# Short convolutions computed at the projection's PSUM tiles, with neighbours' terms accumulated in DRAM, and the last column groups regrouped

## The chip, the cores and the metric

The kernel runs on one core of one Trainium2 chip. The metric is the device time of one execution in microseconds (us); of a kernel the median over its runs is given. All arithmetic is float32; the large matrix products split their operands in two parts (a rounded high part and the rest) and add three products.

## The reference

A two-layer backbone over 2048 tokens of width 1024. Layer 0 is a pooling mixer beside attention; layer 1, which the change concerns, is a Hyena mixer (long convolutions) beside a 2-D Fourier mixing. Cut to what matters:

```python
def short_conv3(u, w, b):
    up = jnp.pad(u, ((0, 0), (1, 1), (0, 0)))
    return up[:, :-2] * w[0] + up[:, 1:-1] * w[1] + up[:, 2:] * w[2] + b

def hyena_mixer(u, conv_w, conv_b, w1, b1, w2, b2, w3, freq, skip):
    uc = short_conv3(u, conv_w, conv_b)                 # 2304 channels
    v, x1, x2 = jnp.split(uc, HY_ORDER + 1, axis=-1)    # 768 channels each
    k = hyena_filters(L, w1, b1, w2, b2, w3, freq)
    z = v.astype(jnp.float32)
    for o, gate_o in enumerate((x1, x2)):
        z = gate_o * (fft_long_conv(z, k[:, o]) + skip[o] * z)
    return z

def odd_mix(h, w_in, w_out, ...):                       # layer 1
    hy_in, hy_gate, fn_in, fn_gate = jnp.split(h @ w_in, ODD_SPLITS, axis=-1)
    yc = hyena_mixer(hy_in, ...)
    yd = fourier_mixer(fn_in, fn_w)
    y = jnp.concatenate([yc * silu(hy_gate), yd * silu(fn_gate)], axis=-1)
    return y @ w_out
```

## The kernel before

**Layout.** Channels lie on the 128 partitions. The 3584 columns of layer 1's input projection are 28 groups `mt` of 128: 0 to 5 are `v`, 6 to 11 `x1`, 12 to 17 `x2`, 18 to 23 the Hyena gate, 24 and 25 the Fourier input, 26 and 27 its gate. Tokens are stored in the order n2 * 128 + n1 for token 16 * n1 + n2, as 16 slots of 128. So a token's neighbours lie in the same column of the slot before and the slot after; only slot 0 and slot 15 have neighbours one column further, in each other. A token block `tb` is four slots, 512 tokens.

**Who orders the work.** The order of the instructions on each engine is written out by a small planner (`Jobs`). `jobs.pe(us)` says how long the matrix products just given will take and lets planned time pass; lanes (`Lane`) hold generators whose `yield us, gap` or `yield event` say how long a piece takes and when the next may come; `jobs.at` gives a function a planned time; `jobs.store` puts a store into SP's queue at the next `jobs.pe`. Planned times only decide the order. On the chip each engine and each DMA queue goes through its own list in order and waits for what an instruction needs. SP's queue carries nearly all loads and stores, POOL's queue those that accumulate (`accum_op=ALU.add`) and some loads.

**Layer 0's end (about 1740 to 2075 us).** `out_half` computes layer 0's output projection; `turn_one` transposes, scales and splits the normalized tokens (`hf`, `ch`); `project0` computes the columns of the four groups FIRST (0, 1, 6, 7) from them, one PSUM bank each, and `keep_cols` copies each bank on ACT into `dev` and stores it to `ud[mt]` in DRAM. Group 0 is treated apart (`first_unit`): its short convolution and the first step of its transform are done at once.

**The projection stage (about 2075 to 2812 us).** 192 steps: six groups of four `mt` (`MGROUPS`), four token blocks, eight blocks of 128 input channels; twelve matrix products a step (L306 to L308), with `dw` (weights) and `dh` (the layer's input) loaded by SP, `dh` three steps ahead (`HL`). After each eighth step `keep_cols` takes the four banks: ACT copies (L1522) or SiLU (L1525) into `dev`, then a store. Between these steps go the long convolutions: twelve units (j, o), each a transform by TensorE matrices and a 16-point transform on DVE (`s1`, `conv_units`, `fft16`), a product with the filter's spectrum (`gK`), and back (`s4`, with the gating of `co`, L1913 and L1917). DVE's part of a unit comes in the order of the units.

**The short convolutions** are done by `conv(n)`, one group after another, on the lane `ctl`: POOL's queue loads the whole group, 1 MB, into `cu` (L1824); ACT computes the middle term with the bias into `co` (L1829) and the first tap into `tap`, half a group at a time in one buffer (L1834); POOL's queue adds `tap` to `co`, SBUF to SBUF (L1837, L1840, L1841); ACT scales `cu` by the last tap in place (L1842) and POOL's queue adds that too (L1844, L1845). `cdone[mt]` releases the gating or the transform that reads `co`. The planned gaps CV0 to CV3 are 14, 12, 8 and 15 us.

**After the projections.** `udone` of the last four groups is set; the Fourier mixing (`hEO`, tables `tab`), the first pass of the output projection for the channels EARLY (added to `x1d` in DRAM from `ox`, L2196), the last units of the long convolutions, and the last pass with the final norm from about 3056 us.

Of the kernel before, what the change touches and what calls it, by code (L numbers as in the profile page):

```python
# [20 lines left out]
P = 128  # L21
D = 1024
# [17 lines left out]
EARLY, LATE = (0, 1, 2, 6, 7), (3, 4, 5)  # L40

# [16 lines left out]
def constants():  # L58
    """Tables that depend on the shapes alone."""
# [58 lines left out]
def sbc(ap, n):  # L118
    """[p, f] -> [p, n, f], the same f for each n."""
    return ap.unsqueeze(1).to_broadcast([ap.shape[0], n, ap.shape[1]])  # L120


def lbc(ap, n):
    """[p, f] -> [p, f, n], each element n times."""
    return ap.unsqueeze(2).to_broadcast([ap.shape[0], ap.shape[1], n])


def fft16(v, X, T, inv, s=None):
    """16-point transforms over the slots of X[p, re/im, 16, C]; T is of the same shape.
# [26 lines left out]
    def stt(out, in0, scalar, op, in1):  # L156
        """in0 already has its factor where s does the products, but for the sign"""
# [28 lines left out]
    def tan(n, *dims):  # L186
        """the slots from n on, times the tangent"""
# [16 lines left out]
    # the second four: slots k * e + b * o for b; 11 and 14 have the other sign  # L204
# [35 lines left out]
def tile_net(ctx, tc, i, k, out, keep=None):  # L240
# [9 lines left out]
    def mv(dst, src, eng=None):  # L250
        """a DMA of float32 words, of either type"""
# [22 lines left out]
    def y1_part(kk):  # L274
        """the place of gated channels of layer 1"""
# [5 lines left out]
    wevd, wod = ([dram(f"w{x}{kk}", (P, 2, D)) for kk in range(KD)] for x in "eo")  # L281
    hdd = dram("hdd", (8, 64, 4, P))
# [30 lines left out]
    class Lane:  # L313
        """pieces for one engine, each of so many us, the next one at least so many later, or after an event"""
# [30 lines left out]
    class Jobs:  # L345
        """the order in which work is given to the engines: matrix products in front, the rest when they are that far"""
# [37 lines left out]
        def until(self, done):  # L384
            """let time pass until done()"""
# [15 lines left out]
    def load_wout(sp, wp, w, kks, dst, gb, wait=4.0, eng=sy, ve=v):  # L401
        """output projection times the gate, in two parts, one tile of rows at a time"""
# [21 lines left out]
    def load_gate(wp, n):  # L424
        """the gate of layer n, the same in every partition"""
# [4 lines left out]
    def rstd_steps(sp, ss, n, tag, scale):  # L430
        """ss [p, n] sums of squares -> 1 / sqrt(ss * scale + eps), with a Newton step after the square root"""
# [13 lines left out]
    def normed_steps(sp, xs):  # L445
        """each slab [p, D] of xs -> each row over its root mean square, in place"""
# [13 lines left out]
    def modulated_steps(sp, pp, xs, gs, sh, emit, lo_eng):  # L460
        """transposed, scaled and shifted, in two parts: emit(m) gives their places"""
# [12 lines left out]
    LASTE, LASTR, GATE2, FOLD1, HALF, SUM0, SUM1, ADDF, FEW, LASTW, IN_C, FFT_N, FFT_LATE, HL, DR, DE, EW0, EW1, SPLIT, SUMMED, QSEL, CV0, CV1, CV2, CV3, COL, NW0, NW1, FIRST_Z, MORE, X0_SQ, X0_STEP, TRAIL, C_EARLY, A_TURN, A_SLOW, A_AHEAD, A_W, A_PACE, LAG0, FOLD, WAIT, AHEAD, LAG, APART, LOW, W_LOAD, W_HIGH, W_LOW, ADDED, SLOW = 0, 0.5, 5, 6, 1.5, 0.2, 1.5, 3, 9, 3.5, 25, 6, 4, 3, 4, 4, 8.0, 2.5, 15, 0.5, 1, 14, 12, 8, 15, 5, 24, 0, 20.0, 8, [7, 7, 11, 11], (0, 0, 0, 0, 2, 2, 2, 2), 11, 1, 2.5, 0.25, 3.5, 4, 1.05, 7, 2, 6.0, 2.5, 5, 5, 2, 6, 6, 4, 8, 1.02  # L474
    # tokens in the order n2 * 128 + n1 for token 16 * n1 + n2
# [5 lines left out]
    FIRST = (0, 1, 6, 7)  # L481
    MGROUPS = [(2, 8, 12, 18), (3, 9, 13, 19), (4, 10, 14, 20), (5, 11, 15, 21), (24, 25, 26, 27), (16, 22, 17, 23)]

    def load_columns(raw, gi, kk, half, eng=sy):
        """128 rows of half of the columns of a group"""
# [5 lines left out]
    with ExitStack() as st, tc.manual_schedule(engines=EVERY):  # L491
# [10 lines left out]
        def load_tb(tb):  # L502
            """a block of tokens, a list of slabs"""
# [14 lines left out]
        def weights(c0, dst):  # L518
            """256 columns of the input projection, in two parts, one tile per 128 rows"""
# [13 lines left out]
        def norm_parts(xs):  # L533
            """the same as normed_steps, in smaller steps"""
# [12 lines left out]
        with ExitStack() as s2:  # L547
# [21 lines left out]
            # the filters' network, on two halves of its input at a time  # L569
# [26 lines left out]
            def load_first(n):  # L596
                """256 columns for the keys, as many for the values"""
# [125 lines left out]
        class Aside:  # L723
            """work that goes between the matrix products, in pieces of so many us of an engine, the next one so many later"""
# [31 lines left out]
        def turn(xs, gs, sh, tiles, lo_eng=(v, v)):  # L756
            """normalized tokens, modulated and turned, in two parts"""
# [12 lines left out]
        def rope_tables(tb):  # L770
            """cos and sin times the norm's gains, for queries and keys"""
# [15 lines left out]
        def heads(raw, ss, nt, tb, nm, dst, col0):  # L787
            """raw [p, nt, 2, HD] in place: ss its sums of squares; normalized over HD, rotated; transposed to dst[head]"""
# [41 lines left out]
        def modulation():  # L830
            """what is left of the modulation: the gate of layer 0, all of layer 1"""
# [51 lines left out]
        def mixer():  # L883
            """the pooling mixer, over halves of n1"""
# [893 lines left out]
    with ExitStack() as st, tc.manual_schedule(engines=EVERY):  # L1778
# [212 lines left out]
        with ExitStack() as ps:  # L1991
# [29 lines left out]
            for mt in MGROUPS[-1]:  # L2021
                udone[mt].t = jobs.now
# [349 lines left out]
```

## Time and profile before

| | |
|---|---|
| median of 3 runs | 3173.34 us (3167.35 to 3176.21) |
| span of the profiled execution | 3162.6 us |
| its own time | not given beside the span; the median lies 10.7 us above the span |
| busy: PE, DVE, ACT, POOL | 2996.1, 2183.2, 1329.8, 1215.5 us |
| DMA | 614.72 MB, mean 194 GB/s |

The span goes from the first to the last instruction of one execution. "Busy" is the time in which an engine ran instructions (matmul ends are modelled); the share of a stage is read from windows of the trace, and who waits for what from the semaphores. `A <- B` in a row of waits means that A's engine stood until B was done. A row of DMA issues gives the tile written and the one read, the queue, the count, the size of one and the median time from issue to landing. q0 is the queue of the DMAs that POOL issues, q1 that of the others.

### The profile page before, as it was taken

How to read it: one execution, taken by the hardware profiler on the slowest of the kernel's cores; microseconds unless marked ns; L12 is line 12 of the kernel's file. 1: busy time of each engine (PE TensorE's matmuls, PEld its weight loads, DVE VectorE, ACT ScalarE, POOL GpSimd, SP SyncE). 2: the span in 40 equal slices, each digit the busy share in tenths (PEclk: the TensorE clock that was granted, in tenths of full speed). 3: DMA queues.
4: the chain of work that ended last, by engine and by line, in shares of the span. 5: the costliest groups of instructions: out<-in, count | busy, mean ns of one | idle time of the engine just before them, and what ended most of it. 6: DMA issues, size and time to landing. Idle time of an engine off the chain costs nothing. (4 is left out here: it accounts for less than half of the span.)

```text
span 3162.6 us, 49927 instructions
## 1 busy us (share of the span) xinstructions
PE 2996.1 (95%) x18121; PEld 2589.2 (82%) x18121; DVE 2183.2 (69%) x4124; ACT 1329.8 (42%) x3130; POOL 1215.5 (38%) x1595
## 2 busy tenths in 40 slices
PE   8999999799999999999999999999989999988799
PEld 4888888699999998999898778777878787874587
DVE  4775437477777777777776443377789797978556
ACT  4444545355555555555556332322323232232123
POOL 3122223027888887878886344001010100101110
PEclk9999999899999999999999999999999999999899
DMA  6466345534444445444443777678899989976875
GB/s 223 157 202 202 125 132 162 182 107 127 121 140 132 128 127 169 121 125 133 117 115 117 250 261 256 242 258 283 275 290 288 293 282 314 275 260 167 233 210 176
DMA packets 425393, 614.72 MB, mean 194 GB/s; under 512 B 140278, under 2 KB 278200, under 8 KB 416698
## 3 DMA queue, kind: packets, MB, share of 16 engines
q1 hardware_dynamic: 399994, 528.43, 51.0%
q0 software_dynamic: 25152, 83.10, 11.2%
q8 instruction: 143, 2.34, 0.3%
q14 instruction: 104, 0.85, 0.1%
HBM read 388.60 MB, written 187.18 MB: 182 GB/s over the span
## 5 line engine op out<-in xcount | busy, mean ns | idle before, releaser
L303 DVE TENSOR_TENSOR pl<-pt,ph 128x512 fp32r<-128x512 f32 (+1 forms) x480 | 299.8, 633 | 137.1 <-ACT ph L300 136.1
L151 DVE TENSOR_TENSOR gB<-gB 128x256 f32<-128x256 f32 (+3 forms) x442 | 351.6, 845 | 51.2 <-ACT gB L1879 47.3
L300 ACT CAST ph<-pt 128x512 fp32r<-128x512 f32 (+1 forms) x480 | 253.5, 556 | 244.7 <-PE pt L1317 242.3
L306 PE MATMUL dacc<-dh,dw 128*128 128x512 f32 x768 | 312.2, 407 | 40.2 <-DMA dh<-h1T 39.5
L1306 ACT ACTIVATE pb<-S,mx 128x512 f32<-128x512 f32 (+1 forms) x480 | 309.7, 656 | 82.7 <-DVE mx L1298 59.4
L307 PE MATMUL dacc<-dh,dw 128*128 128x512 f32 x768 | 304.7, 397 | 0.0
L308 PE MATMUL dacc<-dh,dw 128*128 128x512 f32 x768 | 304.6, 397 | 0.0
L1295 DVE TENSOR_REDUCE mx<-S 128x1 f32<-128x512 f32 (+1 forms) x480 | 279.9, 629 | 18.6 <-DMA kh<-kT0h 14.0
L303 POOL TENSOR_TENSOR wl<-raw,wh 128x256 fp32r<-128x256 f32 x160 | 135.6, 880 | 368.6 <-ACT wh L300 356.7
L1317 PE MATMUL pt<-ident,pb 128*128 128x128 f32 x1728 | 248.0, 275 | 11.2 <-ACT pb L1306 10.9
L151 POOL TENSOR_TENSOR fX<-fT 128x128 f32<-128x128 f32 (+2 forms) x336 | 246.7, 757 | 4.9
L1329 PE MATMUL o<-ph,vh 128*128 128x256 f32 x864 | 233.0, 301 | 1.4 <-ACT ph L300 1.2
L151 POOL TENSOR_TENSOR fT<-fX 128x1024 f32<-128x1024 f32 (+1 forms) x192 | 202.6, 1081 | 49.0 <-ACT fX L1203 44.6
L1317 PEld LDWEIGHTS pt<-ident,pb 128*128 128x128 f32 x1728 | 197.2, 141 | 28.2 <-ACT pb L1306 14.8
L1330 PE MATMUL o<-ph,vl 128*128 128x256 f32 x864 | 216.5, 282 | 1.5 <-DMA vl<-vl 1.5
L306 PEld LDWEIGHTS dacc<-dh,dw 128*128 128x128 f32 x768 | 147.9, 193 | 78.2 <-DMA dh<-h1T 46.7
L306 PE MATMUL S<-kh,qh 128*128 128x512 f32 (+1 forms) x480 | 196.9, 410 | 9.9 <-DMA kl<-kT0l 8.2
L306 PE MATMUL acc<-wh,hh 128*128 128x256 f32 x672 | 197.2, 293 | 3.5 <-ACT qraw L969 2.4
L308 PE MATMUL acc<-wh,hl 128*128 128x256 f32 x672 | 193.1, 287 | 1.2 <-DVE hl L303 0.9
L307 PE MATMUL acc<-wl,hh 128*128 128x256 f32 x672 | 192.8, 287 | 0.9 <-POOL wl L303 0.8
L307 PE MATMUL S<-kl,qh 128*128 128x512 f32 (+1 forms) x480 | 180.4, 376 | 1.1 <-DMA kl<-kT0l 1.0
L308 PE MATMUL S<-kh,ql 128*128 128x512 f32 (+1 forms) x480 | 180.4, 376 | 0.0
(473 smaller groups left out, 7776.5 us busy)
## 6 DMA issues: line engine op xcount, KB each, us to landing
dh<-h1T SPq DMA_DIRECT2D x172, 512.0 KB
dec<-cst_decay_dram SPq DMA_DIRECT2D x96, 256.0 KB
spec<-fX SPq DMA_DIRECT2D x24, 1024.0 KB
dw<-wi SPq DMA_DIRECT2D x48, 512.0 KB
gK<-spec SPq DMA_DIRECT2D x48, 512.0 KB
raw<-in_ev_w_in_dram SPq DMA_DIRECT2D x160, 128.0 KB
u<-dev SPq DMA_DIRECT2D x70, 256.0 KB
cu<-u POOLq DMA_DIRECT2D x17, 1024.0 KB, 8.3
```

Of the source, the lines that this page charges most:

```text
L151: put(out, lambda: v.tensor_tensor(out=out, in0=in0, in1=in1, op=op))
L300: s.copy(hi, src)
L303: lo_eng.tensor_sub(lo, src, hi.bitcast(F32))
L306: pe.matmul(acc, ah, bh, start=first, stop=False)
L307: pe.matmul(acc, ah, bl, start=False, stop=False)
L308: pe.matmul(acc, al, bh, start=False, stop=last)
L1295: v.tensor_reduce(out=B["mx"][:, c : c + 1], in_=S[:, :n], axis=AX.X, op=ALU.max)
L1306: s.activation(B["pb"][:, c * 512 : c * 512 + n], B["S"][c][:, :n], AF.Exp, bias=B["mx"][:, 5:6], accum_out=B["sm"][:, c : c + 1])
L1317: pe.transpose(pt[:, t, :], B["pb"][:, (4 * c + t) * P : (4 * c + t + 1) * P], ident)
L1329: pe.matmul(gr["o"], vh[:, a, :], ph[:, t, :], start=a == 0, stop=False)
L1330: pe.matmul(gr["o"], vl[:, a, :], ph[:, t, :], start=False, stop=False)
```

## The change

The neighbours' terms and the bias are applied to each block of 128 channels by 512 tokens as it leaves PSUM, instead of to a whole group later. Within the block, two slots next to each other are served on DVE; one neighbour at the block's edge is kept in SBUF for the next block (`edges`, `before`), and terms that belong to slots already stored are scaled on ACT (`far`, `low`) and accumulated into `ud[mt]` in DRAM by POOL's queue. The blocks of a group of columns run upwards or downwards in turn (`up`). `conv(n)` is only a load of the finished group. In detail, for groups 2 to 5 and 8 to 17 (comments and docstrings, which the change also removes, and moved blank lines are left out):

```diff
-    MGROUPS = [..., (24, 25, 26, 27), (16, 22, 17, 23)]
+    MGROUPS = [..., (16, 22, 24, 25), (17, 23, 26, 27)]
+    firstd = [dram(f"first{mt}", (P, P)) for mt in range(18)]
-    ... CV0, CV1, CV2, CV3, ... = ... 14, 12, 8, 15, ...
+    ... CV0, CV1, CV2, CV3, CV_N, CV_S, DE_, ... = ... 0.3, 2.5, 6, 10, 5, 1.7, 5, ...

+    def taps(mt):
+        return *(col2[:, 18 * x + mt : 18 * x + mt + 1] for x in range(3)), ud[mt].rearrange("p (a b) -> p a b", a=N2)
+    def add_to(dst, src):
+        g.dma_start(dst, src, accum_op=ALU.add)
     def keep_cols(jobs, ep, mt, acc, tb, up=True):
...
-        if mt < 18 or mt in (24, 25):
+        if 0 < mt < 18:
+            s.copy(ev, acc)
+            convlane[0].add(short_conv(jobs, ep, mt, ev.rearrange("p (a b) -> p a b", a=4), tb, up))
+        elif mt < 18 or mt in (24, 25):
             s.copy(ev, acc)
             jobs.store((ud[mt] if mt < 18 else fid[mt - 24])[:, bl], ev)

+    def short_conv(jobs, ep, mt, u, tb, up):
+        w0, w1, w2, o = taps(mt)
+        n0 = 4 * tb
+        first, final_ = (0, NB - 1) if up else (NB - 1, 0)
+        wn, wf = (w0, w2) if up else (w2, w0)
+        next_, other = (3, 0) if up else (0, 3)
+        own, of = (slice(1, 4), slice(0, 3)) if up else (slice(0, 3), slice(1, 4))
+        yield 0.0, CV0
+        mid = ep.tile([P, 4, P], F32, tag="ev", name="dm")
+        s.activation(mid, u, AF.Identity, bias=..., scale=w1)
+        far = nextfar()
+        s.mul(far, u, wf)
+        yield 0.0, CV_S
+        v.scalar_tensor_tensor(out=mid[:, own], in0=u[:, of], scalar=wn, in1=mid[:, own], op0=ALU.mult, op1=ALU.add)
+        if tb == first:
+            edges[mt] = ep.tile([P, P], F32, tag="eb", name="deb", bufs=4)
+        else:
+            v.tensor_add(mid[:, other], mid[:, other], edges[mt])
+        s.mul(edges[mt], u[:, next_], wn)
+        jobs.lanes[0].took(jobs.now, 0.8)
+        def put():
+            sy.dma_start(o[:, n0 : n0 + 4], mid)
+            if tb == first:
+                sy.dma_start(firstd[mt], far[:, other])
+        def more():
+            x = int(tb == first)
+            if up:
+                add_to(o[:, n0 - 1 + x : n0 + 3], far[:, x:])
+            else:
+                add_to(o[:, n0 + 1 : n0 + 5 - x], far[:, : 4 - x])
+            if tb == final_:
+                to0, to15 = (edges[mt], firstd[mt]) if up else (firstd[mt], edges[mt])
+                add_to(o[:, 0, 1:], to0[:, : P - 1])
+                add_to(o[:, 15, : P - 1], to15[:, 1:])
+                del edges[mt]
+        jobs.at(jobs.now + CV1, 0.0, put)
+        jobs.at(jobs.now + CV2, 0.0, more)
```

`fars` are four such blocks in the room of the former `cu`, used in turn. `ep` has five buffers (`DE_`) instead of four in the projection stage. For the groups 1, 6 and 7 of FIRST, straight from PSUM:

```diff
+        def first_conv(n, mt, u, tb):
+            w0, w1, w2, o = taps(mt)
+            n0 = 4 * tb
+            mid = ep.tile([P, 4, P], F32, tag="ev", name="cm")
+            s.activation(mid, u, AF.Identity, bias=..., scale=w1)
+            low = ep.tile([P, P], F32, tag="cl", name="cl", bufs=3)
+            s.mul(low, u[:, 0], w2)
+            def rest():
+                for to, of, w in ((slice(1, 4), slice(0, 3), w0), (slice(0, 3), slice(1, 4), w2)):
+                    v.scalar_tensor_tensor(out=mid[:, to], in0=u[:, of], scalar=w, in1=mid[:, to], op0=ALU.mult, op1=ALU.add)
+                if tb:
+                    v.tensor_add(mid[:, 0], mid[:, 0], before[n])
+                else:
+                    before[n] = ep.tile([P, P], F32, tag=f"cb{n}", name="cb", bufs=1)
+                s.mul(before[n], u[:, 3], w0)
+                dve.took(jobs.now, 1.4)
+                jobs.store(o[:, n0 : n0 + 4], mid)
+                if tb == 0:
+                    jobs.store(firstd[mt], low)
+                jobs.at(jobs.now + 4.0, 0.0, edge)
+            def edge():
+                if tb:
+                    add_to(o[:, n0 - 1], low)
+                if tb == NB - 1:
+                    add_to(o[:, 0, 1:], before[n][:, : P - 1])
+                    add_to(o[:, 15, : P - 1], firstd[mt][:, 1:])
+            jobs.at(jobs.now + 1.3, 0.0, rest)
-            hf = sp.tile([P, 512], F32, tag="hf", name="hf", bufs=1)
+            hf = sp.tile([P, 4, P], F32, tag="zT", name="hf").rearrange("p a b -> p (a b)")
```

And what reads the result:

```diff
         def conv(n):
             mt = convs[n]
             yield udone[mt]
             yield cdone[convs[n - 1]]
-            u = per.tile([P, N2, P], F32, tag="u", name="cu")
-            QU.dma_start(u, ud[mt].rearrange("p (a b) -> p a b", a=N2))
-            yield 0.0, CV0
             if mt in room:
                 yield room[mt]
             o = cout[mt] = (per if mt < 6 else ct).tile([P, N2, P], F32, tag="ct", name="co")
-            s.activation(o, u, AF.Identity, bias=..., scale=...)
-            ...
-            g.dma_start(o[:, 15, : P - 1], u[:, 0, 1:], accum_op=ALU.add)
+            QU.dma_start(o, ud[mt].rearrange("p (a b) -> p a b", a=N2))
             yield 0.0, CV3
             cdone[mt].t = jobs.now
...
-                if x % GS == 0 and x:
+                if x % GS == CV_N and x > GS:
                     for mt in MGROUPS[gi - 1]:
                         udone[mt].t = jobs.now
...
+            jobs.until(lambda: not edges)
             for mt in MGROUPS[-1]:
                 udone[mt].t = jobs.now
```

More of the change, by code (lines that the diff above doesn't have):

```diff
@@ L40 @@
 EARLY, LATE = (0, 1, 2, 6, 7), (3, 4, 5)
+FIRST = (0, 1, 6, 7)
 BLOCK = [
@@ L479, in tile_net @@
     EVERY = {ET.PE, ET.DVE, ET.Activation, ET.Pool, ET.SP}
-    FIRST = (0, 1, 6, 7)
-    MGROUPS = [(2, 8, 12, 18), (3, 9, 13, 19), (4, 10, 14, 20), (5, 11, 15, 21), (24, 25, 26, 27), (16, 22, 17, 23)]
+    MGROUPS = [(2, 8, 12, 18), (3, 9, 13, 19), (4, 10, 14, 20), (5, 11, 15, 21), (16, 22, 24, 25), (17, 23, 26, 27)]
     def load_columns(raw, gi, kk, half, eng=sy):
@@ L1647, in project0 @@
                         s.copy(u0[0][:, 4 * tb : 4 * tb + 4, :], accs[n].rearrange("p (a b) -> p a b", a=4))
+                    elif n == 0:
+                        keep_cols(jobs, ep, 0, accs[n], tb)
                     else:
-                        keep_cols(jobs, ep, FIRST[n], accs[n], tb)
+                        first_conv(n, FIRST[n], accs[n].rearrange("p (a b) -> p a b", a=4), tb)
                 if 0 in ns:
@@ L1654, in project0 @@
                 jobs.pe(0.65 * len(ns))
+        before = {}
+        def first_conv(n, mt, u, tb):
+            w0, w1, w2, o = taps(mt)
+            n0 = 4 * tb
+            mid = ep.tile([P, 4, P], F32, tag="ev", name="cm")
+            s.activation(mid, u, AF.Identity, bias=col2[:, PK2["cb"] + mt : PK2["cb"] + mt + 1], scale=w1)
+            low = ep.tile([P, P], F32, tag="cl", name="cl", bufs=3)
[20 more added lines that the diff above has]
+            jobs.at(jobs.now + 1.3, 0.0, rest)
         columns = [Event() for _ in range(NB)]
@@ L1828, in conv @@
             o = cout[mt] = (per if mt < 6 else ct).tile([P, N2, P], F32, tag="ct", name="co")
-            s.activation(o, u, AF.Identity, bias=col2[:, PK2["cb"] + mt : PK2["cb"] + mt + 1],
-                         scale=col2[:, 18 + mt : 19 + mt])
-            yield 0.0, 2.2
-            for a in (0, 8):
-                t = sp.tile([P, 8, P], F32, tag="tap", name="tap", bufs=1)
-                s.mul(t, u[:, a : a + 8], col2[:, mt : mt + 1])
-                yield 0.0, 1.2
-                if a == 0:
-                    g.dma_start(o[:, 1:9], t, accum_op=ALU.add)
-                    yield 0.0, CV1
-                else:
-                    g.dma_start(o[:, 9:], t[:, :7], accum_op=ALU.add)
-                    g.dma_start(o[:, 0, 1:], t[:, 7, : P - 1], accum_op=ALU.add)
-            s.mul(u, u, col2[:, 36 + mt : 37 + mt])
-            yield 0.0, CV2
-            g.dma_start(o[:, :15], u[:, 1:], accum_op=ALU.add)
-            g.dma_start(o[:, 15, : P - 1], u[:, 0, 1:], accum_op=ALU.add)
+            QU.dma_start(o, ud[mt].rearrange("p (a b) -> p a b", a=N2))
             yield 0.0, CV3
@@ L1991, in tile_net @@
         with ExitStack() as ps:
-            ep = pool(ps, "d_e", DE)
+            ep = pool(ps, "d_e", DE_)
+            u8 = per.tile([P, N2, P], F32, tag="u", name="far")
+            convlane.append(jobs.lane())
+            fars.extend(u8[:, 4 * x : 4 * x + 4] for x in range(4))
             pm = pool(ps, "d_ps", 1, PSUM)
@@ L2264, in tile_net @@
             jobs.flush()
-            fg = sp.tile([P, D], F32, tag="tap", name="fg", bufs=1)
+            jf = per.tile([P, 2, D], F32, tag="u", name="jk")
+            junk, fg = jf[:, 0], jf[:, 1]
             sy.dma_start(fg, i["final_g"].rearrange("(o d) -> o d", o=1).to_broadcast([P, D]))
-            junk = per.tile([P, D], F32, tag="u", name="jk")
             eps = modc[:, 12:13]
```

12 lines of the change are left out of this document (9 added, 3 removed).

## The prediction

> **What bounds the kernel now.** I read the page's first lines, then one table of stages, then who waits for whom in the stage that the change rewrites, then single rows around the longest stop there.
>
> ```profile
> span 3162.6 us, 49927 instructions
> ...
> PE 2996.1 (95%) x18121; PEld 2589.2 (82%) x18121; DVE 2183.2 (69%) x4124; ACT 1329.8 (42%) x3130; POOL 1215.5 (38%) x1595
> ```
>
> PE is the bound over the whole span: 166.5 us are all that it idles (its matmul ends are modelled, so this is a floor). The change removes no matrix product, so it can only win back idle time and the slow clock that follows it. By stages, in the columns PE, weight loads, DVE, ACT, POOL, granted clock, DMA share, GB/s:
>
> ```profile
> 1740.00:2060.00 320.00, 306.59 (x1483) 252.99 (x1482) 127.44 (x212) 97.44 (x194) 100.77 (x125) 0.98 0.70 251
> 2190.00:2812.00 622.00, 585.14 (x3133) 499.93 (x3131) 514.12 (x852) 182.34 (x231) 60.35 (x75) 0.98 0.91 287
> 2812.00:2945.00 133.00, 118.80 (x506) 78.93 (x507) 108.88 (x190) 35.36 (x58) 11.31 (x14) 0.92 0.71 210
> 2945.00:3056.00 111.00, 94.22 (x422) 75.95 (x420) 64.58 (x108) 25.47 (x46) 25.54 (x31) 0.92 0.90 225
> ...
> 2060.00:2812.00 752.00, 704.00 (x3674) 597.89 (x3672) 619.41 (x1015) 215.75 (x274) 71.16 (x89) 0.97 0.90 284
> ```
>
> The first row is layer 0's output projection with the columns FIRST, the last row the projection stage with most of the long convolutions. It has 48 us of PE idle and a clock of 0.97, which is 0.03 x 752 = 22.6 us more, some of it inside the idle time. From 2812 to 3056 (Fourier mixing, first output pass) PE idles 14.2 + 16.8 = 31.0 us. The waits of the projection stage (us in total, times, longest):
>
> ```profile
> POOL co L1837 <- ACT tap L1834: 215.1, 14, 23.9
> ...
> ACT tap L1834 <- DMA co<-tap: 64.2, 8, 10.9
> DVE co L1913 <- PE go L1904: 51.6, 13, 6.9
> ...
> DVE gB L151 <- ACT gB L1879: 47.3, 5, 19.1
> ...
> PE dacc L306 <- DMA dh<-h1T: 39.5, 18, 8.3
> ```
>
> 39.5 of the 48 us are PE waiting for its moving operand `dh`. Why it is late shows around the longest of these stops (ACT, then SP's queue, then PE):
>
> ```profile
> 2304.45 1.16 ACT L1834 ACTIVATE tap<-cu,col 128x1024 f32<-128x1024 f32 x1 [8.51 <-DMA co<-tap]
> ...
> 2307.55 1.54 ACT L1522 COPY dev<-dacc 128x512 f32<-128x512 f32 x3
> ```
> ```profile
> 2308.14 1.66 SPq L252 DMA_DIRECT2D u<-dev  x3
> ```
> ```profile
> 2168.66 0.79 PE L306 MATMUL dacc<-dh,dw 128*128 128x512 f32 x1 [4.06 <-DMA dh<-h1T]
> ...
> 2327.79 0.79 PE L306 MATMUL dacc<-dh,dw 128*128 128x512 f32 x1 [8.29 <-DMA dh<-h1T]
> 2328.38 0.63 PE L307 MATMUL dacc<-dh,dw 128*128 128x512 f32 x1
> ...
> 2477.43 0.79 PE L306 MATMUL dacc<-dh,dw 128*128 128x512 f32 x1 [6.50 <-DMA dh<-h1T]
> ```
>
> ACT stands 8.5 us in `conv` because the single buffer `tap` is still being read by an accumulating DMA; the PSUM copies queue behind it on ACT; SP's queue stands at the stores of these copies; the loads of `dh` stand behind the stores. The DMA engines are 0.90 busy besides. So two causes meet, and the short convolutions feed both.
>
> **The change part by part.** *DMA time.* The queues' shares in 2060 to 2812, the accumulations there, and the one accumulation into DRAM that the trace has, with its queue in 2945 to 3058, where it is nearly alone:
>
> ```profile
> q1 hardware_dynamic: 57863, 164.99, 60.9%
> q0 software_dynamic: 12672, 48.15, 28.4%
> ...
> cu<-u POOLq DMA_DIRECT2D x15, 1024.0 KB, 8.4
> ...
> co<-cu POOLq DMA_DIRECT2D x14, 960.0 KB, 9.3
> ...
> co<-tap POOLq DMA_DIRECT2D x15, 512.0 KB, 7.8
> co<-tap POOLq DMA_DIRECT2D x15, 448.0 KB, 8.1
> ```
> ```profile
> q0 software_dynamic: 4176, 7.60, 42.7%
> ...
> x<-ox POOLq DMA_DIRECT2D x30, 256.0 KB, 5.9
> ```
>
> q1 moves 164.99 MB in 0.609 x 752 = 458 us, 0.360 MB a us. q0 has 213.6 us for 48.15 MB. Its 15 loads of 1 MB and a table of 2 MB by the code, 17.8 MB, would take 49 us at q1's rate, which leaves 164 us for 30.3 MB of accumulation, 0.185 MB a us. Accumulating into DRAM gave 7.60 MB in 0.427 x 113 = 48.3 us, 0.157 MB a us. After the change each of the 14 channel groups of this stage accumulates 960 KB + 2 x 63.5 KB = 1.11 MB instead of 2.10: 15.6 MB, 99 us at the DRAM row's rate. The stores and the 1 MB load stay; `firstd` adds 0.9 MB, 3 us. The DMA engines are relieved of 164 - 99 - 3 = 62 us, and the share falls from 0.90 to about 0.82.
>
> *PE's wait for dh, 39.5 us.* The stop of ACT on the accumulating DMA goes entirely (`tap` is gone); the crowding falls by a tenth, but the start of a group of columns still loads weights and `dh` together. I take two thirds away: **-26 us** (ends 0 and -39.5; nearer the far end because of the chain shown). Late next: the same loads at the group boundaries, and the new stores below.
>
> *The clock.* After the stop at 2327.8 matmuls of 128x512 take 0.79 and 0.63 us in the rows above. If half of the 22.6 us is outside the idle time, and goes as the stops go, it is **-7** (0 to -15). The Trainium skill, TensorE: Matmul & The Clock Gate, Part 1, says that the clock falls to half after an idle window of about 3.4 us and comes back after as long a busy one; by it only stops that reach that length, the three quoted, would cost 1.7 us each, 5 us in all, and the sum would be 2 to 5 us less good. The rows bear out the halving.
>
> *DVE.* Per channel group: four multiply-adds over 384 elements and three additions over 128, where before it did nothing. Nearest rows (the last from layer 0's stage):
>
> ```profile
> L162 DVE SCALAR_TENSOR_TENSOR gB<-gB,gB 128x256 f32<-128x256 f32 x170 | 61.6, 418 | 0.0
> ...
> L162 DVE SCALAR_TENSOR_TENSOR gB<-gB 128x128 f32<-128x128 f32 x68 | 16.6, 285 | 0.0
> ```
> ```profile
> L1690 DVE SCALAR_TENSOR_TENSOR z<-u,col,z 128x512 f32<-128x512 f32 x3 | 2.3, 751 | 0.3 <-ACT z L1695 0.2
> ```
>
> A 384 lies between 418 and 751 ns, 0.58 in the middle: 56 x 0.58 + 42 x 0.285 = 44 us (35 to 54). DVE has 514 of 622 us busy: its cover is 17%, and it shrinks to 10%. But DVE also gets time back, since the short convolutions no longer hold up the long ones:
>
> ```profile
> 2143.48 10.49 DVE L151 TENSOR_TENSOR gB<-gB 128x2048 f32<-128x2048 f32 x8 [19.09 <-ACT gB L1879]
> ...
> 2235.90 4.50 DVE L151 TENSOR_TENSOR gB<-gB 128x2048 f32<-128x2048 f32 x2 [16.37 <-ACT gB L1879]
> ...
> 2382.65 10.49 DVE L151 TENSOR_TENSOR gB<-gB 128x2048 f32<-128x2048 f32 x8 [6.34 <-ACT gB L1879]
> ```
>
> These three, 41.8 us, are transforms whose input came late; the loads of `conv` now need 10 planned us where the chain of one took 53.6 (14 + 2.2 + 1.2 + 12 + 1.2 + 8 + 15). POOL shows that chain running without a pause, about 50 us each, from the first load to the last:
>
> ```profile
> 2067.05 0.54 POOL L1824 DMA_DIRECT2D cu<-u  x1 [85.80 <-DMA u<-dev]
> ...
> 2865.60 0.56 POOL L1824 DMA_DIRECT2D cu<-u  x1 [7.81 <-issue]
> ```
>
> So the transforms start about 42 us earlier and carry 44 us more: they end where they ended. I count **0** for DVE's own time; without that cover it would be up to 44.
>
> *SP's queue.* 56 plain stores become 56 stores `put` that wait for ACT, DVE's multiply-add and addition; behind them stand `dh`, `dw`, `gK`. No row shows this wait. Below, it is no longer than the stop of ACT it replaces (a gain, counted above); above, each of the 16 token blocks with three short convolutions stops PE for as long as DVE is behind. A step takes about 752 / 192 = 3.9 us and `dh` is fetched three steps ahead, 11.7 us, of which a 512 KB transfer in the rows above needs 7.8: some 4 us are free. The plan puts a store 2.5 us after its multiply-add, and DVE still has gaps in which it waits for PE (51.6 us above) to catch up. I take **+6** (0 to +50, 3 us a block).
>
> *ACT and POOL.* A scale of 2048 took 2.1 us in three pieces before; now it is per block three shorter operations, no more than 12 x 0.59 = 7.1 against 6.4 us per group; ACT is 29% busy, and what waits behind it waits less. POOL issues seven DMAs where it issued six, with 60 of 622 us busy. Its conv load now stands behind accumulations that wait for `put`; 10 us of plan cover it. **0**, up to +5 if that cover is gone.
>
> *Layer 0's stage.* 3 groups x 4 blocks x (2 x 0.58 + 0.285) = 17 us on DVE, which has 127 of 320 busy; only the last two blocks lie on PE's path, and there the second buffer for `hf` gives back. **+1** (-4 to +6).
>
> *After the projections.* Two short convolutions used to run there, the last load at 2865 above; q0 took 25.9% of 133 us = 34 us of DMA time beside table loads for which PE waits:
>
> ```profile
> q0 software_dynamic: 2160, 7.41, 25.9%
> ```
> ```profile
> 2812.00 1.12 PE L1865 MATMUL gt__29498<-ident,co 128*128 128x128 f32 x4 [6.06 <-DVE co L1913]
> ...
> 2927.93 9.74 PE L2128 MATMUL hEO<-tab,PQ 128*128 128x512 f32 x16 [3.62 <-DMA tab<-cst_dftl_dram]
> ```
>
> Of 31 us idle I take back **-10** (+10 to -25): the first pass stays behind its accumulation into `x1d`, whose DMA is unchanged. Waiting for `edges` to be empty and the later `udone` reorder the planner's time: **+2** (0 to +8). The regrouping lets group 16 be ready earlier, which only keeps the chain from waiting: 0.
>
> Sum: -26 - 7 + 0 + 6 + 0 + 1 - 10 + 2 = -34 us. The span of 3162.6 would be 3129; the median of the runs shown, 3173.3, lies 10.7 above that span, so the time is **3139 us**.
>
> **The rivals.** *More goes than I say*: all of dh's wait (-39.5), the whole clock term (-15), -20 behind, +4 for the rest: -70, 3103 us. For it: both causes are one chain; against: 0.82 of the DMA engines is still much. *Nothing gained*: the accumulations into DRAM come in 256 KB pieces; at 5.9 us each against 9.3 for 960 KB they are in flight 4 x 5.9 = 23.6 us per group against 7.8 + 8.1 + 9.3 = 25.2, so if time in flight and not bytes crowds `dh`, its wait stays, clock too: +6 + 1 - 5 + 2 = +4, 3177 us, no change. The Trainium skill, DMA: Bandwidth & Descriptors, under Bandwidth, has this as a rule: batch transfers to 1 MiB or more. The two DRAM and SBUF rates above, 0.157 and 0.185, agree with it only weakly. *Slower*: `put` stops SP's queue because DVE, at 90%, is behind. From a lateness of 4 us PE waits; at 7 us, 3 us in each of 16 blocks, 48 us, with 8 for the clock; with -26 - 7 - 10 + 1 + 2 still there, +16: 3189 us. For it: one queue for everything; against: DVE's 51.6 us of waiting for PE.
>
> **How the numbers follow.** Forecast 0.52, more 0.22, nothing 0.14, slower 0.12. About 0.3%, 9.5 us, is what a measurement of this kernel can tell from no change. Faster 0.72 (forecast and more, less an edge), same 0.15, slower 0.13. The range takes in the larger gain and the case of no gain, 3095 to 3186; the forecast's own is 3115 to 3160.
>
> **What would show it.** Right: no wait of ACT for an accumulating DMA; PE's wait for `dh` at about 13 us; DMA share near 0.82 and DVE near 90% in the projection stage; the first three DVE gaps gone. Wrong: SP's queue waiting for DVE at `put`; the dh wait at 30 us or more; DVE gaps that move behind 2812 into PE.

## The result, and the profile after

The kernel after takes 3209.26 us (median of 4 runs, 3197.45 to 3212.94), the one before beside it 3173.35: a ratio of 1.0107, interval 1.0091 to 1.0123. It is 36 us slower; 3139 us had been forecast, and the time lies above the range. The profiled execution took 3208.97 us, its span 3207.2. Single executions that took over 5000 us are left out of the times and ratios below.

The first lines of the page after:

```profile
span 3207.2 us, 50230 instructions
...
PE 3000.9 (94%) x18121; PEld 2594.8 (81%) x18121; DVE 2241.2 (70%) x4255; ACT 1329.3 (41%) x3254; POOL 1229.7 (38%) x1609
```

PE does the same work (3000.9 against 2996.1 us busy) and idles 206.3 us instead of 166.5. Where, is read by stages, with the first and last product of `dacc`, those of `hEO` and the first product of the last pass as borders (us):

| | before | after | later place, no reservation (last experiment) |
|---|---|---|---|
| start to first `dacc` | 2075.1 | 2096.1 | 2081.2 |
| projections (`dacc`) | 726.9 | 732.6 | 701.2 |
| to `hEO` | 50.4 | 54.2 | 52.3 |
| Fourier mixing (`hEO`) | 84.7 | 77.3 | 70.7 |
| first output pass | 119.0 | 137.0 | 113.9 |
| last pass | 106.5 | 110.0 | 106.4 |

So the 44.6 us between the spans are +21.0 at the start, +5.7, +3.8, -7.4, +18.0 and +3.5. Rows of stages of before, then of after (columns as in the prediction: PE, weight loads, DVE, ACT, POOL, clock, DMA share, GB/s):

```profile
2075.00:2802.00 727.00, 685.65 (x3568) 582.27 (x3569) 602.06 (x994) 205.80 (x262) 68.93 (x86) 0.97 0.91 289
...
2937.00:3056.00 119.00, 102.22 (x472) 82.91 (x470) 72.08 (x123) 27.19 (x51) 25.54 (x31) 0.93 0.89 229
```
```profile
2096.00:2829.00 733.00, 685.85 (x3537) 581.36 (x3538) 593.94 (x1002) 213.39 (x370) 79.64 (x97) 0.97 0.84 264
...
2960.00:3097.00 137.00, 102.40 (x440) 82.01 (x438) 99.65 (x175) 27.13 (x50) 25.63 (x31) 0.88 0.81 207
```

The DMA share fell as forecast (0.84; 0.82 was forecast), and PE got nothing for it. DVE is the surprise: it has 47 us of short convolutions more to do in the projection stage and is busy *less*, 593.94 against 602.06 us. So some 55 us of other work, most of it the long convolutions', have left the stage. Behind the projections DVE is busy 38 us more than before (281.96 against 244.20), 27 of them in the first output pass; most of the rest runs ahead of the stage, in the longer start. The waits of the stage say why, and the groups of DVE's two new operations give their price:

```profile
POOL u L1525 <- DMA u<-dm: 440.7, 29, 33.4
ACT dev L1533 <- PE dacc L310: 246.5, 20, 22.6
DVE dm L1557 <- ACT dm L1553: 107.3, 48, 10.6
...
PE dacc L308 <- DMA dh<-h1T: 34.9, 21, 4.2
```
```profile
L1557 DVE SCALAR_TENSOR_TENSOR dm<-dev,col,dm 128x384 f32<-128x384 f32 x56 | 34.6, 618 | 111.6 <-ACT dm L1553 107.3 <-DMA u<-dm 2.7 <-DMA sg<-dev 1.5
...
L1561 DVE TENSOR_TENSOR dm<-dm,deb 128x128 f32<-128x128 f32 x42 | 11.9, 285 | 0.0
```

DVE stands 107.3 us, in 48 waits at the 56 multiply-adds, for ACT's product `dm`. DVE is not behind; it is too early. One block shows it (DVE, ACT, SP's queue, PE of after):

```profile
2311.30 0.62 DVE L1557 SCALAR_TENSOR_TENSOR dm<-dev,col,dm 128x384 f32<-128x384 f32 x1
2311.84 0.29 DVE L1561 TENSOR_TENSOR dm<-dm,deb 128x128 f32<-128x128 f32 x1
2314.77 0.62 DVE L1557 SCALAR_TENSOR_TENSOR dm<-dev,col,dm 128x384 f32<-128x384 f32 x1 [2.65 <-ACT dm L1553]
```
```profile
2313.92 0.82 ACT L1553 ACTIVATE dm<-dev,col 128x512 f32<-128x512 f32 x1 [1.36 <-DMA sg<-dev]
```
```profile
2312.20 5.79 SPq L1566 DMA_DIRECT2D u<-dm  x3
2318.08 2.01 SPq L253 DMA_DIRECT2D dh<-h1T  x1
```
```profile
2325.05 0.79 PE L308 MATMUL dacc<-dh,dw 128*128 128x512 f32 x1 [4.24 <-DMA dh<-h1T]
```

The planner puts the three multiply-adds of a block into DVE's order right behind one another. ACT has not come that far with the block (it waits 1.36 us for a buffer); DVE stands, with a transform waiting behind it; the three stores (`put`) keep SP's queue for 5.79 us, the loads of `dh` come only after them, and PE stops for 4.24 us.

At the start another order of the work costs time in a like way. DVE, ACT and PE of after:

```profile
2079.18 0.61 DVE L1734 SCALAR_TENSOR_TENSOR cm<-cacc,col,cm 128x384 f32<-128x384 f32 x1
...
2093.49 0.61 DVE L1734 SCALAR_TENSOR_TENSOR cm<-cacc,col,cm 128x384 f32<-128x384 f32 x1
2095.35 0.28 DVE L1736 TENSOR_TENSOR cm<-cm,cb 128x128 f32<-128x128 f32 x1
```
```profile
2095.67 0.37 ACT L1739 ACTIVATE cb<-cacc,col 128x128 f32<-128x128 f32 x1 [5.93 <-DVE cm L1736]
```
```profile
2096.14 0.76 PE L308 MATMUL dacc<-dh,dw 128*128 128x512 f32 x1 [14.84 <-ACT cb L1739]
```

The last block's `rest` stands between the pieces of the first long convolution's transforms, so its last addition starts only at 2095.35. ACT's edge product overwrites the tile `cb` that this addition reads, so it comes after it; it reads the PSUM bank as well, and the first product of the projections waits 14.84 us for the bank. Some 5 us of the 21 appear ahead of the first changed instruction (layer 0's output projection starts at 1775.3 instead of 1769.9), as a difference between the two executions.

### The profile page after: what moved, and what is told of

It reads as the page before. It is cut to its first block, busy times and chain, and to the rows that moved or that the text cites. A ratio compares the mean times of both kernels' runs of the same rounds, so it can differ in the third digit from the quotient of the medians.

```text
span 3207.2 us, 50230 instructions
## 1 busy us (share of the span) xinstructions
PE 3000.9 (94%) x18121; PEld 2594.8 (81%) x18121; DVE 2241.2 (70%) x4255; ACT 1329.3 (41%) x3254; POOL 1229.7 (38%) x1609
## 5 line engine op out<-in xcount | busy, mean ns | idle before, releaser
L308 PE MATMUL dacc<-dh,dw 128*128 128x512 f32 x768 | 310.3, 404 | 49.8 <-DMA dh<-h1T 34.9
L1525 POOL DMA_DIRECT2D u<-far x56 | 53.2, 985 | 590.9 <-DMA u<-dm 466.2
```

Source lines behind the costliest of these rows:

```text
L308: pe.matmul(acc, ah, bh, start=first, stop=False)
```

## The experiments

All times are medians; ratios are to the kernel before, run beside each experiment, with their intervals. The medians of the kernel before lie between 3168 and 3176 us, so a few us between two experiments say nothing. "A plan of 2.5 us" means the planner's time.

**The start.** For the last block ACT copies the banks of groups 1, 6 and 7 to SBUF, and makes its edge product ahead of DVE's part.

```diff
+            if tb == NB - 1:
+                s.copy(c, u)
+                u = c
...
+                s.mul(edge_, u[:, 3], w0)     # ahead of rest()
```

> The changed kernel, but for the last token block of layer 0's stage ACT copies each PSUM bank of groups 1, 6 and 7 to SBUF at once, and the short convolution reads that copy; ACT no longer stands behind DVE there. Theory A (the start): PE's 14.8 us wait for the first projection product goes, and with it the 18.5 us in which DVE waits for gK behind SP's stores of cm; 3209 falls by 15 to 20 us, to about 3192. Theory B (DVE's chain of long convolutions is what the end hangs on, and the start matters only through it): the same only if DVE's first unit is earlier too; if just PE's wait goes, it comes back behind the projections and the time stays at 3205 to 3209.

3198.87 us, 1.0074 [1.0049, 1.0099]. The wait of 14.84 us is gone and the first `dacc` is at 2083.1, 13 us earlier; PE's wait for `dh` rises from 34.9 to 43.5 us. Some 10 us of the loss is the start, less than the 15 to 20 that were expected; the rest stays.

**DVE's part left out**, then **done on data that waits for nothing.** The first run drops both DVE operations of `short_conv` in the projection stage and their reservation; the second does the same operations, as many and as large, but for 12 of the 14 groups on a constant table, and keeps the reservation. In neither do the stores of these groups wait for DVE any more.

```diff
-        v.scalar_tensor_tensor(out=mid[:, own], in0=u[:, of], scalar=wn, in1=mid[:, own], ...)
-            v.tensor_add(mid[:, other], mid[:, other], edges[mt])
+        v.scalar_tensor_tensor(out=sc[:, own], in0=d_[:, of, 0], scalar=wn, in1=d_[:, own, 1], ...)   # second run
+                v.tensor_add(sc[:, other], d_[:, 4, 0], d_[:, 5, 0])
```

> The changed kernel with DVE's multiply-add and addition of the short convolutions left out in the projection stage (the terms of neighbours within a block and of the block before are missing); everything else, stores and accumulations too, stays. Theory B (DVE is held up there, by the work of 46 us or by standing for ACT's dm, 107 us): the long convolutions end some 45 us earlier, 3155 to 3170 us. Theory C (DMA: dh waits because of the stores and the accumulations into DRAM): no change, 3200 to 3210, dh's wait stays at 35 us.

> The changed kernel with the same operations of DVE, of the same sizes and at the same places in its order, but for 12 of the 14 groups they read a constant table and write a scratch tile, so they wait for nothing that PE or ACT makes (the neighbours' terms within a block are missing there). It parts the two halves of theory B. B1 (standing: DVE, which takes its list in order, waits at these operations until PE has finished the block): nearly all of what the run without them gains is gained here too, 3165 to 3175. B2 (work: 46 us more on an engine that is nearly full): as the changed kernel, 3200 to 3209.

3171.43 us, 0.9992 [0.9975, 1.0008], and 3181.47 us, 1.0024 [1.0008, 1.0039]. DVE's part, with its reservation, costs 38 us, and 28 of them go although DVE does all of the work: they are its waiting, or that of the stores behind it, which this run doesn't tell apart. The projection stage of the second run:

```profile
2092.00:2801.00 709.00, 679.69 (x3534) 578.46 (x3535) 591.19 (x1002) 209.15 (x369) 79.99 (x97) 0.98 0.86 273
```

The first output pass is 114 us long in the first of the two (its projection stage 721) and still 136 in the second. So what the first gains beyond the second it gains there: through the work that is gone, or its reservation. The last experiment points to the reservation.

**The accumulations into DRAM left out** (those of `far`; the edges' small ones stay).

```diff
-                add_to(o[:, n0 - 1 + x : n0 + 3], far[:, x:])
+                pass
```

> The changed kernel without the accumulations of far into DRAM in the projection stage (these terms are missing; the two small ones at a group's end stay). Theory C: 13 MB of accumulation less, PE's wait for dh falls from 35 to under 15 us and the time by 20 us or more, 3180 to 3190. Theories A and B: dh's wait falls a little, the time by 0 to 8 us, 3200 to 3209.

3181.71 us, 1.0030 [1.0016, 1.0045]: 28 us. The wait for `dh` falls from 34.9 to 15.3 us. The run takes away the traffic and also much of POOL's standing for stores, so the 28 us need not be the traffic alone. The row of DMA issues of after shows the time in flight, 8.3 us where the prediction had taken 5.9 from the output pass:

```profile
u<-far POOLq DMA_DIRECT2D x41, 256.0 KB, 8.3
```

**The kernel before without short convolutions** (each group is only loaded; groups other than 0 lack the convolution).

```diff
-            u = per.tile(...); QU.dma_start(u, ...); s.activation(o, u, ...); s.mul(t, ...); g.dma_start(o..., accum_op=ALU.add) ...
+            QU.dma_start(o, ud[mt].rearrange("p (a b) -> p a b", a=N2))
```

> The kernel before with the short convolutions left out for every group but group 0: conv only loads the projected columns (planned gap 10 us, as in the changed kernel). It is what the removal alone is worth, with nothing in its place. If removal is worth what the prediction said (dh, clock and the time behind the projections, 43 us) or what the three partial runs sum to (3209 - 38 - 28 - 10 = 3133): 3125 to 3140 us. If the time of before hangs on something else (the long convolutions' chain on DVE, the first output pass): 3155 to 3170.

3110.52 us, 0.9811 [0.9789, 0.9833]; PE's wait for `dh` falls from 39.5 to 3.2 us, the stage from 727 to 683 us at a clock of 1.00:

```profile
2079.00:2762.00 683.00, 679.84 (x3680) 586.43 (x3678) 617.27 (x1021) 125.89 (x216) 7.44 (x15) 1.00 0.75 265
```

The old short convolutions cost some 60 us, more than the 43 that the prediction hoped to win (26 + 7 + 10) and more than the experiment's own expectation. That they made `dh` late and the clock slow was right; what came in their place cost nearly 100.

**POOL in DVE's place** (ACT scales `dev`, POOL adds), and a second version of it with the mended start, in which POOL also adds `far` within the block and only one slot in four is accumulated in DRAM, with stores, accumulations and loads planned later.

```diff
-        v.scalar_tensor_tensor(out=mid[:, own], in0=u[:, of], scalar=wn, in1=mid[:, own], ...)
+        s.mul(u, u, wn)
+        g.tensor_add(mid[:, own], mid[:, own], u[:, of])
+        g.tensor_add(mid[:, of], mid[:, of], far[:, own])     # second version
```

> The changed kernel with the multiply-add and the addition of the projection stage's short convolutions moved from DVE: ACT scales dev in place by the tap, POOL adds; POOL then waits for PE's block instead of DVE. Theory B (DVE): as the run without DVE's part, 3170 to 3180. Rival: POOL takes its list in order too and stands 466 us for stores before it accumulates, so these additions, the stores behind them and SP's queue come late: 3195 to 3215.

> The changed kernel with the start mended as in the first run, POOL in DVE's place, and POOL also adding far within the block, so that only one slot of four (64 KB instead of 256 KB) is accumulated into DRAM; stores planned 5 us, accumulations 14 us after the products. If the three costs found (start 10, DVE 38, accumulation 28, of which three quarters are 21) add up: 3209 - 69 = 3140 us, faster than both kernels. If POOL's own standing takes their place: 3175 or more.

3299.31 us, 1.0406 [1.0383, 1.0429], and 3276.43 us, 1.0354 [1.0303, 1.0405], both far above what was expected. POOL stands for ACT as DVE did, SP's queue for POOL (148 us at `put` in the first, from 2100 to 2800), and PE waits 102.1 us for `dh`. Groups of the first of them:

```profile
L1558 POOL TENSOR_TENSOR dm<-dm,dev 128x384 f32<-128x384 f32 x55 | 72.1, 1311 | 552.8 <-ACT dev L1557 552.8
L163 DVE SCALAR_TENSOR_TENSOR gB<-gB,gB 128x256 f32<-128x256 f32 x176 | 70.7, 457 | 0.0
```

An addition of 384 takes 1311 ns, 2.1 times DVE's multiply-add (618). The Trainium skill, GPSIMD Engine Reference, 4.1 Engine selection, says about twice for two inputs, and the trace agrees. DVE's own row beside it rose from 418 to 457 ns; the same page of the Trainium skill, Specifications, has the two sharing their way to SBUF.

**The old grouping of the last columns** in the kernel after.

```diff
-    MGROUPS = [..., (16, 22, 24, 25), (17, 23, 26, 27)]
+    MGROUPS = [..., (24, 25, 26, 27), (16, 22, 17, 23)]
```

> The changed kernel with the old grouping of the last columns: (24, 25, 26, 27), (16, 22, 17, 23). The prediction counted 0 for the regrouping: 3204 to 3214. If it does matter, group 16's gate comes only with the last group and the last two short convolutions crowd the end: 3215 to 3230.

3209.68 us, 1.0123 [1.0096, 1.0151]: no difference from the kernel after. The regrouping is worth 0, as predicted.

**`tap` on POOL in the kernel before**, so that POOL and not ACT stands for the accumulating DMA.

```diff
-                s.mul(t, u[:, a : a + 8], col2[:, mt : mt + 1])
+                g.tensor_scalar(out=t, in0=u[:, a : a + 8], scalar1=col2[:, mt : mt + 1], scalar2=None, op0=ALU.mult)
```

> The kernel before, with the two products per group that go into the buffer tap taken from ACT to POOL (28 products of 128x1024), so that only POOL stands until the accumulating DMA has read the buffer. Nothing else is changed, and the DMA traffic is the same. Theory A (the prediction's first chain: ACT's stop holds back PSUM copies, the stores behind them and the loads of dh): PE's wait for dh falls from 39.5 us to 20 or less and the time from 3173 to about 3150. Rival B (the traffic crowds dh, ACT's stop is a bystander): the wait stays at 33 us or more and the time at 3168 to 3180. Rival C (POOL's products of some 3 us slow DVE's own rows beside them): over 3180.

3175.50 us, 1.0007 [0.9992, 1.0022]. ACT's 64.2 us at `tap` are gone and the wait for `dh` is 46.6 us, not less. But with POOL's product of 3.64 us ACT now waits 100.2 us for POOL at the last scaling of `cu`: its stop has moved and not gone. So the run doesn't decide between ACT's stop and the traffic; the run with loads alone took away both.

**Both costs left out together, start mended**: no DVE part, no accumulation of `far`.

> The changed kernel with the start mended, and both of the suspected costs of the projection stage left out together: DVE's multiply-add and addition (the output lacks these terms) and the accumulations of far into DRAM (lacking as well). Loads, ACT's products and all plain stores stay. Each alone gave about 10, 38 and 28 us. Theory A (costs add): 3209 - 10 - 38 - 28 = 3133 us, PE's wait for dh 5 us or less, and what is left above the run with loads alone, 3110, is the stores, ACT's products and the small terms. Rival B (both act through the one wait of PE for dh and overlap): 3145 to 3160, since either run alone already halved that wait.

3134.81 us, 0.9867 [0.9841, 0.9893], where 3133 was expected if they add. In this order of the work the losses add.

**The same work, later.** The multiply-add comes 5.2 us of plan after ACT's product instead of 1.7, then 7.4 us, and the store and the accumulation behind it as much later; the start is mended in both. A lane may run 2.5 us ahead of the plan, so at 1.7 it was put into DVE's order at once.

```diff
-    ... CV0, CV1, CV2, CV3, CV_N, CV_S, DE_ ... = ... 0.3, 2.5, 6, 10, 5, 1.7, 5, ...
+    ... CV0, CV1, CV2, CV3, CV_N, CV_S, DE_ ... = ... 0.3, 2.5, 6, 10, 5, 5.2, 5, ...     # then 7.4
```

> The changed kernel with the start of the last block mended and DVE's multiply-add planned 3.5 us later after ACT's product (1.7 us of plan to 5.2), so that DVE no longer stands in its order for a block that PE has not finished; the store follows later by as much. Theory A (DVE standing for PE costs the long convolutions their lead): DVE's wait for ACT's dm falls from 107 us to under 50, the stage from the first to the last projection product from 739 to about 715, the time from 3199 to about 3175. Rival B (what costs is the DVE work and the traffic, and the standing only fills idle time): the wait falls and the time stays within 8 us of 3199.

> The same run with the multiply-add another 2.2 us of plan later (5.2 to 7.4). Theory A (what is left of DVE's wait for ACT's dm, 26 us, still costs the long convolutions): that wait falls below 10 us, the stage of the projections from 692 to about 680, the time to about 3150. Rival B (what is left is inside DVE's idle time, and a later store only keeps buffers and SP's queue longer): 3158 to 3172.

3160.53 us, 0.9951 [0.9934, 0.9968], and 3141.97 us, 0.9913 [0.9894, 0.9933]. No work is left out, and both are faster than the kernel before. The groups of PE's products and of the multiply-add in the stage, at 5.2:

```profile
L308 PE MATMUL dacc<-dh,dw 128*128 128x512 f32 x768 | 306.2, 399 | 20.5 <-DMA dh<-h1T 19.7 <-issue 0.7
...
L1557 DVE SCALAR_TENSOR_TENSOR dm<-dev,col,dm 128x384 f32<-128x384 f32 x55 | 33.8, 614 | 24.2 <-ACT dm L1553 24.2
```

The stage falls from 739 us, in the run that mends the start alone, to 692, then to 683 at 7.4 (`dh` 13.0 us, DVE's wait 6.8). The rows of the stage, with the start alone and at 7.4:

```profile
2083.00:2822.00 739.00, 683.59 (x3534) 579.83 (x3535) 617.05 (x1047) 214.37 (x372) 82.50 (x101) 0.97 0.84 264
```
```profile
2085.00:2768.00 683.00, 668.29 (x3534) 571.08 (x3535) 621.26 (x1060) 213.55 (x372) 82.33 (x101) 1.00 0.91 286
```

PE does the same products in both. It idles 14.7 us instead of 55.4, 30.5 of the difference at `dh` (43.5 to 13.0), and it is busy 15.3 us less at a clock of 1.00 instead of 0.97. The first output pass stays long, 141 and 131 us. There PE stops for the last long convolution:

```profile
3040.21 1.19 PE L1995 MATMUL go<-idft,gB 128*128 128x128 f32 x4 [16.08 <-DVE gB L152]
```

**Without the reservation.** `took` tells the planner that DVE is taken for 0.8 us per block. It goes, at 5.2 and then at 7.4; the work stays.

```diff
-        jobs.lanes[0].took(jobs.now, 0.8)
```

> The run with the later multiply-add (3161 us), and the planner's reservation of 0.8 us per block for it on DVE's lane taken out; DVE still does the work. It asks why the first output pass grew from 119 us before to 141. Theory A (DVE's real 46 us of short-convolution work push the transforms of the last unit behind the projections): the first pass stays at 135 to 145, PE's last wait for DVE's gB at about 16 us, the time within 8 us of 3161. Rival B (the reservation of 45 us of plan pushes them back, the work itself would find room): the first pass falls to 125 or less, and the time to 3145.

> The two last edits together: the multiply-add 7.4 us of plan after ACT's product, and no reservation for it on DVE's lane. Each alone gave 15 to 19 us against the run with 5.2 (3161). Theory A (they act on different stages, the later place on the projections, the missing reservation on the first output pass): they add, 3128 us. Rival B (without the reservation DVE was 94% busy in the projection stage, which is full, so a later place of the multiply-add has nothing left to give): 3138 to 3150.

3145.52 us, 0.9926 [0.9911, 0.9940], and 3131.40 us, 0.9878 [0.9861, 0.9894]. The first output pass is 114 us long in both. The reservation, 56 x 0.8 = 45 us of plan, had put the last convolution's transforms behind the projections. Without it they come earlier: the projection stage grows from 692 to 714 and from 683 to 701 us, since PE does some 144 products more in it, and idles 24.4 and 15.9 us there, little more than with the reservation (21.3 and 14.5). Transforms' groups on DVE in the first pass, with the reservation (at 5.2), then without:

```profile
L152 DVE TENSOR_TENSOR gB<-gB 128x256 f32<-128x256 f32 (+3 forms) x60 | 47.8, 847 | 0.4
```
```profile
L152 DVE TENSOR_TENSOR gB<-gB 128x256 f32<-128x256 f32 (+3 forms) x20 | 16.2, 847 | 0.2
```

The last kernel, with both edits, beats before and after. Its projection stage and first pass, its groups, and the block of columns that was shown of after (SP's queue, then DVE):

```profile
2081.00:2782.00 701.00, 684.91 (x3678) 587.39 (x3679) 671.56 (x1151) 219.05 (x384) 82.19 (x102) 1.00 0.89 284
2905.00:3019.00 114.00, 95.12 (x409) 74.98 (x407) 52.74 (x87) 27.07 (x50) 25.48 (x31) 0.93 0.91 234
```
```profile
L308 PE MATMUL dacc<-dh,dw 128*128 128x512 f32 x768 | 305.6, 398 | 14.2 <-DMA dh<-h1T 13.1 <-issue 0.7 <-ACT dev L1533 0.4
...
L1557 DVE SCALAR_TENSOR_TENSOR dm<-dev,col,dm 128x384 f32<-128x384 f32 x55 | 33.7, 612 | 0.0
```
```profile
2297.10 0.32 SPq L253 DMA_DIRECT2D dh<-h1T  x1
2299.16 0.32 SPq L1565 DMA_DIRECT2D u<-dm  x1
2299.52 0.43 SPq L253 DMA_DIRECT2D dw<-wi  x1
2300.35 0.32 SPq L253 DMA_DIRECT2D dh<-h1T  x1
...
2305.57 0.33 SPq L1565 DMA_DIRECT2D u<-dm  x1
```
```profile
2298.25 0.61 DVE L1557 SCALAR_TENSOR_TENSOR dm<-dev,col,dm 128x384 f32<-128x384 f32 x1
2298.78 0.29 DVE L1561 TENSOR_TENSOR dm<-dm,deb 128x128 f32<-128x128 f32 x1
2298.98 4.68 DVE L152 TENSOR_TENSOR gB<-gB 128x2048 f32<-128x2048 f32 x3
2303.58 0.61 DVE L1557 SCALAR_TENSOR_TENSOR dm<-dev,col,dm 128x384 f32<-128x384 f32 x1
```

The same multiply-adds of 0.61 us now lie one by one between transforms and wait for nothing; in this block the stores leave one by one between loads of `dh`. DVE is busy 671.56 of 701 us, 96%, and PE hardly waits for it: 13.1 of PE's 16 us of idle time are `dh`. ACT does wait for DVE (153 us at the edge product), and so does SP's queue at `put`, in after first and then in the last kernel:

```profile
SPq L1566 <- DVE dm L1561: 64.5, 37, 3.4
SPq L1566 <- DVE dm L1557: 8.7, 13, 0.9
```
```profile
SPq L1565 <- DVE dm L1561: 70.5, 24, 7.5
SPq L1565 <- DVE dm L1557: 30.6, 8, 8.9
```

That is 101 us in the kernel that wins against 73 in the one that lost. So the sum of SP's waits at `put` does not tell the good order from the bad one here; PE's wait for `dh` (13.1 against 34.9 us) and the clock (1.00 against 0.97) do.

## Why the prediction was wrong

It forecast 3139 us, and the change as it stood gave 3209. Three orders of work make up the distance to the last kernel: the start 10 us (3209 to 3199), the place of the multiply-add with its store and accumulation 57 us (3199 to 3142), the reservation 11 to 15 us. Mended, the same change gives 3131 us, 8 from the forecast; that nearness is partly luck, since a clock term twice as large makes up for most of the gain after the projections, which did not come. The range ended at 3186, short of the prediction's own rival "slower" at 3189. By the prediction's steps:

- **DVE, 0 us: the step that failed.** The work was priced well: 618 and 285 ns, 34.6 + 11.9 = 46.5 us against 44. What it left out is that an operation in an engine's order also costs the time until its operand is there, with everything behind it: 107.3 us of standing here, of which the run on constant data puts some 28 into the kernel's time. It asked whether DVE would be behind and found it had gaps to catch up; DVE was ahead instead. A row that could have warned stands in it: DVE waited 51.6 us for PE, a possible sign that the planner's time already ran ahead of PE, so that an operation on PE's newest bank, placed at once behind ACT's product, might wait as well. The forecast that the first three gaps would go came true, and the gain was stood away at `dm`.
- **The wait for `dh`, -26 us.** 39.5 to 34.9 in after, instead of 13. The size is right in the last kernel, 13.1 us. Its reason stays open: the run meant to free ACT of its stop only moved the stop to another line, and `dh` stayed late.
- **The clock, -7.** 0.97 as before in after; 1.00 in the last kernel, where PE is busy 13.4 us less for its 18121 products (2996.1 to 2982.7), twice the term. In before four further stops at `dh`, of 2.53 to 3.28 us, were followed by products of 0.80 and 0.63 us like the three quoted ones, where after a stop of 1.37 us the second took 0.39; so more than those three carried a slow clock.
- **SP's queue, +6.** The mechanism of the rival "slower" is what the shown block has, with another reason: `put` stops SP's queue not because DVE is full but because it stands. All three signs of being wrong appeared: SP's queue waiting at `put`, 34.9 us for `dh`, and PE waiting for DVE behind the projections, up to 10.5 us at once. The first of them is larger still in the last kernel. The 7.8 us that the sum took for a load of `dh` are from the row of an accumulating DMA between SBUF tiles; no row gives the time of `dh`. The later place moved DVE's operation, the store and the accumulation together, so how much of the 57 us went through SP isn't told apart. By the run on constant data, 28 go with DVE's waiting and that of the stores for it; how the others arise isn't shown.
- **Layer 0's stage, +1 (-4 to +6).** Mis-sized: a wait of 14.84 us, some 10 of it in the kernel's time. The sum counted 17 us of work on an idle DVE, and did not ask what of the next stage stands between the pieces in DVE's order while a PSUM bank is held.
- **After the projections, -10.** The short convolutions' traffic did go (`hEO` 84.7 to 77.3), but the first pass rose by 18 us through transforms put off. In the last kernel the three stages from the projections to the last pass are 17 us shorter (254.1 to 236.9), but PE has 16 us less to do in them (216.9 to 200.8 busy), since transforms come earlier. Its idle time there goes from 37 to 36 us: the 10 us of this term were not won back.
- **The planner's time, +2.** It looked at `edges` and `udone` and not at `took`, which cost 15.0 us at 5.2 (3160.53 to 3145.52) and 10.6 at 7.4.
- **DMA time.** The share fell to 0.84 (0.82 was forecast); it is 0.89 in the last kernel, which moves the same traffic in less time. The rival "nothing gained" had a point: without the accumulations 28 us went, but in the order in which DVE stood. The last kernel, which does all the work, stands at 0.9878, the early order without both at 0.9867, within one another's intervals. What leaving the accumulations out of the last order would give wasn't run.
- **ACT and POOL, regrouping: 0.** POOL's 440.7 us at the accumulations hold only the loads of `conv` behind them, for which none of the stage's larger waits is; the regrouping gave 0.

What stays open: the 21 us between the last kernel (3131) and the run with loads alone (3111), and whether a still later place would give more.

## What to carry to other kernels

When work moves to an engine whose instructions come in a written order, ask not only how long it takes and whether the engine has time, but when its operand is ready beside the plan: an operation placed too early stops everything behind it, and shows as an engine that got less busy with more to do. A run that leaves work out prices it in the present order only: DVE's part and the accumulations cost 38 and 28 us here, and an order that kept both came to the same time as the early order without them. Nor is the sum of a queue's waits a verdict: SP's stood longer at `put` in the faster kernel. Look at the reservations of a planner as at work, for they move other work just as far.

## What the runs showed of the hardware

- An accumulating DMA of 256 KB into DRAM landed after 8.3 us (median) in the projection stage of after, at a DMA share of 0.84, but after 6.7 us in that of the last kernel at 0.89, and after 5.9 in the output pass of before at 0.90. The share alone doesn't say how long it takes.
- POOL's product by a scalar over 128x1024 took 3636 ns (a rough figure, as all of POOL's) where ACT's took 1143 (the run with `tap` on POOL, and before).
- DVE at 96% of a stage left PE's waits for it near nothing (last kernel), though ACT and SP's queue waited for it: when it stood counted more than how full it was.
